# Five pairs with seven products in 13 of 15 linears of a decoder layer, with all their weight sums read from memory

## The chip, the cores and the metric

The kernel runs on one core of one Trainium2 chip. The metric is the device time of one execution, in microseconds (us). The engines are named as in the profile: PE is TensorE (matmuls; PEld its weight loads), DVE is VectorE, ACT is ScalarE, POOL is GpSimd, SP is SyncE. SP issues most DMA transfers on one queue (q1, hardware), POOL issues on another (q0, software).

## The reference

One decoder layer over 272 tokens (16 meta tokens and 256), width D = 2048, in fp32: a SwiGLU feed-forward part with F = 5632, then differential attention and a short convolution side by side, merged by gates, then a second SwiGLU part, then a norm. Cut to what matters:

```python
def swiglu_ffn(h, w_gu, w_down):
    gate, up = jnp.split(h @ w_gu, 2, axis=-1)
    return (jax.nn.silu(gate) * up) @ w_down

s = s + 0.5 * swiglu_ffn(rms_norm(s, norm_ffn1), ffn1_w_gu, ffn1_w_down)
h = rms_norm(s, norm_mix)
q, k, v, b_gate, c_gate, u = jnp.split(h @ w_in, splits, axis=-1)
y_att, y_conv = diff_attention(q, k, v, ...), short_conv_mixer(b_gate, c_gate, u, conv_w)
z = jnp.einsum('blnw,nwd->blnd', jnp.stack([y_att, y_conv], axis=2), w_branch)
s = s + jnp.sum(sigmoid(h @ w_gate) * z, axis=2) @ w_out
s = s + 0.5 * swiglu_ffn(rms_norm(s, norm_ffn2), ffn2_w_gu, ffn2_w_down)
return rms_norm(s, norm_final)[:, N_META:]
```

The weights come from HBM; by their shapes they are 394 MB.

## The kernel before

**Products.** A product of fp32 matrices is made of three matmuls: each operand is split in a high part, rounded to the type that PE takes (fp32r), and the rest. ACT makes the high part of a weight block ("wh", a cast), DVE subtracts it from the block ("wl"), and PE adds up activation-high x wh, activation-low x wh and activation-high x wl (`product`, L555 to L563). Pools: three buffers each of wh and wl (`W_BUFS`), eight of raw blocks of 512 KB (`ST_BUFS`, tag "st"), 28 of the activation tiles (`N_ACT`, tag "act"), eight of tiles for evictions (`ev`).

**Stages.** The first feed-forward part and w_in (to about 1130 us) run through `linear` (L311): one block of two 128-row chunks of weights after the other, 272 tokens wide, each with a load on SP, a cast, a subtraction and the matmuls. The steps of the attention are placed between blocks. Gates and branches (g, z, to about 1390), w_out (o, to about 1483) and the second feed-forward part run through `stream` (L664).

**stream.** It takes a list of slots. At each slot n it writes out the preparation of slot n + 2 (loads on SP, casts, subtractions), then the products of slot n, then steps hung on that slot, and then at most `room` steps from a list `todo` (evictions and the like, on DVE). DVE's instructions stay in the order in which they are written there (`Chain`, `dve`), so they wait for one another; SP's loads go in order too. PE's order is made by the scheduler.

**Two kinds of pairs.** The second feed-forward part is in three thirds of four, four and three groups of 512 columns of F. Each third has its "pg" linears (`w_gu`: 512 gate columns and 512 up columns of a group, together one product of 2x2 blocks) and two "pd" linears (`w_down`). A pg linear goes over eight pairs of 128-row chunks of weights (a pd linear of a third over eight or six). A pair is one of two kinds, by a letter in a string:

- D (`direct`, L565): two slots, 8 products, 24 matmuls of 128x512. Each slot loads 512 KB ("st").
- S (`mixed`, L594): four slots (raw, sums, sums2, single), seven products of sums of blocks in place of eight, 21 matmuls. It needs the raw left blocks "sr", one right block of "sx", and two tiles of sums of weights, "ta" and "tb". Sums of activations are made once ("xf", "ma", "mb", in `combine` and `combining`).

The strings are `HALF` (pg, four S), `TURNED` with `ORDER` (pd of the first two thirds, four S) and `SHORT` (pd of the last third, two S; the last linear of all is D throughout).

**Sums of weights.** ta and tb are made in one of two ways. On the spot: both blocks are loaded whole and DVE makes four additions of 128x512. Or from memory: a `Store` (L267) has made them long before, for a list of units, and the S pair loads ta and tb as it loads weights. In every string one S pair (the third in a linear) is summed on the spot; the others, 47 in all, are units. Beside these, the 12 S pairs of w_gate are summed on the spot.

**The Store.** `tick` is called once for each block of `linear`. Every sixth block (`STEP`) it loads a unit's two blocks "ur" and "un" (512 KB each) through SP into two st buffers, three blocks later it makes the four additions on DVE into two more st buffers "ua" and "ub", and POOL issues the two stores.

Of the kernel before, what the change touches and what calls it, by code (L numbers as in the profile page):

```python
# [9 lines left out]
F32 = mybir.dt.float32  # L10
# [5 lines left out]
P = 128  # L16
D = 2048
SEQ = 256
NMETA = 16
T = SEQ + NMETA  # L20
# [15 lines left out]
N_ACT = 28  # L36
# [6 lines left out]
HALF = "DDDSSDSS"  # L43
TURNED = "DSDSDSDS"
ORDER = (0, 2, 4, 1, 3, 6, 5, 7)
SHORT = "DDDSDS"
STEP = 6
# [4 lines left out]
def decoder_layer(ctx: ExitStack, tc: tile.TileContext, t, out):  # L52
# [54 lines left out]
    grow = const.tile([DC, P], F32, name="grow")  # L107
# [16 lines left out]
    vrows = const.tile([NV, P], F32, name="vrows")  # L124
# [11 lines left out]
    lamv = const.tile([P, 4, HD], F32, name="lamv")  # L136
# [34 lines left out]
    def make_lam():  # L171
        lprod = tmp.tile([P, 2, HD], F32, tag="lprod", bufs=1, name="lprod")
# [46 lines left out]
    class Norm:  # L219
# [5 lines left out]
        def add(self, c):  # L225
            first = self.ssq is None
            if first:
                self.ssq = tmp.tile([P, T], F32, tag="ssq", name="ssq")
            sq = self.ssq if first else tmp.tile([P, T], F32, tag="sq", name="sq")
# [4 lines left out]
        def end(self):  # L234
# [3 lines left out]
            ms = tmp.tile([P, T], F32, tag="ms", bufs=1, name="ms")  # L238
# [16 lines left out]
    def rsqrt(out_, ms, shape, name):  # L255

        a = tmp.tile([P, T], F32, tag="rsa", bufs=1, name="rsa" + name)[:, : shape[1]]
# [9 lines left out]
    class Store:  # L267


        def __init__(self):  # L270
            self.units, self.kept, self.count, self.v = [], {}, -DC // KB, None

        def want(self, w, r0, c0, c1):
            key = (w.tensor.name, r0, c0)
            self.kept[key] = [spill.tile([P, 2 * GW], F32, name=f"sums{len(self.kept)}{n}") for n in "ab"]
            self.units.append((w, r0, c0, c1, self.kept[key]))
# [4 lines left out]
        def tick(self):  # L281
            n = self.count % STEP
# [3 lines left out]
            if n == 0 and self.units:  # L286
                w, r0, c0, c1, _ = self.units[0]
                self.v = [raw_tile(n) for n in ("ur", "un")]
                for tl, cq in zip(self.v, (c0, c1)):
                    nc.sync.dma_start(  # L290
                        out=tl, in_=w[r0 : r0 + 2 * P, cq : cq + GW].rearrange("(c p) f -> p c f", p=P)
                    )
            if n == STEP // 2 and self.v:
                kept = self.units.pop(0)[-1]
                (r, x), self.v = self.v, None
                ta, tb = raw_tile("ua"), raw_tile("ub")
                added(nc.vector, r, x, ta, tb)
                for tl, to in zip((ta, tb), kept):
# [1123 lines left out]
```

## Time and profile before

| | us |
|---|---|
| median of 3 runs (2188.74 to 2189.27) | 2189.15 |
| the profiled execution, its own time | 2188.72 |
| its span, first to last instruction | 2186.9 |
| first feed-forward part and w_in, to about | 1130 |
| g and z, to about | 1390 |
| o, to about | 1483 |
| second feed-forward part, to about | 2160 |

The profiled execution lies 1.8 us above its span and 0.4 us below the median. In the profile "x9" counts instructions; a group of the page has its busy time, the mean of one in ns, and the idle time of the engine ahead of it with what ended that. Matmuls overlap, so that the length of one (some 0.39 us for 128x512) is not the time it takes of PE; that is read from the distance of starts. The name pgC stands for the accumulators C11, C12 and C21 of a pg linear, pgD for D22, pgP for P1, P5, P6 and P7, which only S pairs fill.

### The profile page before, as it was taken

To read this page: it belongs to the slowest core of one execution; us is meant where nothing else is said; L and a number is where in the kernel's file an instruction comes from. 1 tells how busy PE (TensorE), PEld (TensorE's weight loads), DVE (VectorE), ACT (ScalarE), POOL (GpSimd) and SP (SyncE) were. 2 spreads that over 40 slices of the span, in tenths; PEclk is the share of its full clock that TensorE was granted. 3 is DMA by queue.
4 is the path that set the end of the run, shared out by engine and by line. 5 is a ranking of instruction groups with operands and counts; after the bars stand their busy time and mean duration, and the time that the engine had idled before them with its cause. 6 is when DMAs were issued, how large, how long until landed. Compare 5 with 4: busy or idle time off the path is not lost.

```text
span 2186.9 us, 34858 instructions
## 1 busy us (share of the span) xinstructions
PE 2173.7 (99%) x13450; PEld 1955.7 (89%) x13450; DVE 1643.5 (75%) x2214; ACT 1109.3 (51%) x1431; POOL 60.6 (3%) x119
## 2 busy tenths in 40 slices
PE   9999999999999999999999999999999999999998
PEld 8999999999999999999988888888878888888886
DVE  7767665566766767666777787768888988888888
ACT  6434333333433444444445555556666566655665
POOL 0000000000000000000000000000000000000000
PEclk9999999999999999999999999999999999999999
DMA  7787888879888988744556665656777877878874
GB/s 238 263 309 275 294 295 288 301 261 317 302 276 287 320 294 303 260 145 135 167 162 212 212 207 190 211 180 216 250 239 258 280 238 259 273 244 277 282 244 154
DMA packets 240966, 542.09 MB, mean 248 GB/s; under 512 B 18564, under 2 KB 18624, under 8 KB 240800
## 3 DMA queue, kind: packets, MB, share of 16 engines
q1 hardware_dynamic: 225184, 484.25, 66.5%
q0 software_dynamic: 15232, 54.96, 6.7%
q8 instruction: 105, 1.72, 0.3%
q10 hardware_dynamic: 384, 0.66, 0.1%
q14 instruction: 61, 0.50, 0.1%
HBM read 486.18 MB, written 53.61 MB: 247 GB/s over the span
## 4 chain that ended last, share of the span: by engine, by line
PE 98%; ACT 1%; DVE 1%; DMA 1%; issue 0%; DVEq 0%
PE pgC L560 12%; PE pdC L560 7%; PE pgP L560 6%; PE gC L560 5%; PE pd L346 4%; PE pu L346 4%; PE pu L344 4%; PE pd L344 4%; PE pu L345 4%; PE pd L345 4%; PE pg L346 4%; PE pg L344 4%; PE pg L345 4%; PE zC L560 3%; PE o L709 3%; PE pgD L560 3%
## 5 line engine op out<-in xcount | busy, mean ns | idle before, releaser
L331 ACT CAST wh<-st 128x1024 fp32r<-128x1024 f32 x352 | 369.6, 1051 | 566.9 <-PE pd L345 134.8
L332 DVE TENSOR_TENSOR wl<-st,wh 128x1024 fp32r<-128x1024 f32 x352 | 429.6, 1222 | 273.8 <-ACT wh L331 273.2
L84 DVE TENSOR_TENSOR wl<-st,wh 128x1024 fp32r<-128x1024 f32 x246 | 299.3, 1220 | 85.2 <-ACT wh L504 78.2
L504 ACT CAST wh<-st 128x1024 fp32r<-128x1024 f32 x238 | 247.4, 1053 | 184.2 <-PE o L709 39.9
L344 PE MATMUL pg<-h,wh 128*128 128x272 f32 x704 | 202.8, 289 | 1.7 <-ACT wh L84 1.4
L344 PE MATMUL pu<-h,wh 128*128 128x272 f32 x704 | 203.2, 289 | 0.0
L346 PE MATMUL pd<-m,wl 128*128 128x272 f32 x704 | 203.0, 288 | 0.0
L346 PE MATMUL pu<-h,wl 128*128 128x272 f32 x704 | 203.0, 288 | 0.0
L344 PE MATMUL pd<-m,wh 128*128 128x272 f32 x704 | 203.0, 288 | 0.0
L345 PE MATMUL pu<-h,wh 128*128 128x272 f32 x704 | 202.4, 288 | 0.0
L345 PE MATMUL pd<-m,wh 128*128 128x272 f32 x704 | 202.4, 287 | 0.0
L345 PE MATMUL pg<-h,wh 128*128 128x272 f32 x704 | 201.4, 287 | 0.0
L346 PE MATMUL pg<-h,wl 128*128 128x272 f32 x704 | 199.7, 289 | 0.0
L560 PE MATMUL pgC<-wh,h 128*128 128x512 f32 x528 | 163.3, 391 | 0.0
L344 PEld LDWEIGHTS pg<-h,wh 128*128 128x128 f32 x704 | 132.3, 188 | 2.6 <-ACT wh L84 2.6
L504 ACT CAST wh<-ta 128x1024 fp32r<-128x1024 f32 x74 | 77.9, 1052 | 108.3 <-DVE ta L84 72.7
L345 PEld LDWEIGHTS pg<-h,wh 128*128 128x128 f32 x704 | 132.8, 189 | 0.0
L345 PEld LDWEIGHTS pu<-h,wh 128*128 128x128 f32 x704 | 132.7, 189 | 0.0
L345 PEld LDWEIGHTS pd<-m,wh 128*128 128x128 f32 x704 | 132.7, 189 | 0.0
L346 PEld LDWEIGHTS pu<-h,wl 128*128 128x128 f32 x704 | 132.5, 188 | 0.0
L346 PEld LDWEIGHTS pd<-m,wl 128*128 128x128 f32 x704 | 132.5, 188 | 0.0
L344 PEld LDWEIGHTS pu<-h,wh 128*128 128x128 f32 x704 | 132.2, 188 | 0.1
(479 smaller groups left out, 5162.0 us busy)
## 6 DMA issues: line engine op xcount, KB each, us to landing
st<-in_ffn_w_gu_dram SPq DMA_DIRECT2D x176, 512.0 KB, 5.9
st<-in_ffn_w_down_dram SPq DMA_DIRECT2D x140, 512.0 KB, 6.2
st<-in_w_in_dram SPq DMA_DIRECT2D x96, 512.0 KB, 4.4
st<-in_ffn_w_gu_dram SPq DMA_DIRECT2D x176, 256.0 KB, 4.3
sr<-in_ffn_w_gu_dram SPq DMA_DIRECT2D x44, 512.0 KB, 4.2
st<-in_w_gate_dram SPq DMA_DIRECT2D x40, 512.0 KB, 4.7
ur<-in_ffn_w_gu_dram SPq DMA_DIRECT2D x33, 512.0 KB, 7.8
un<-in_ffn_w_gu_dram SPq DMA_DIRECT2D x33, 512.0 KB, 5.0
```

Source lines behind the costliest of these rows:

```text
L84: r = f(*a, **k)
L331: act_.copy(out=wh[:, :m, :], in_=sw)
L332: dve_.tensor_sub(wl[:, :m, :], sw, wh[:, :m, :].bitcast(F32))
L344: nc.tensor.matmul(a, wh[:, i, f], act.part(c, 0, t0, t1), start=first, stop=False)
L345: nc.tensor.matmul(a, wh[:, i, f], act.part(c, 1, t0, t1), start=False, stop=False)
L346: nc.tensor.matmul(a, wl[:, i, f], act.part(c, 0, t0, t1), start=False, stop=last)
L504: nc.scalar.copy(out=wt[0][:, : sw.shape[1], :], in_=sw)
L560: nc.tensor.matmul(ps[:, f0:f1], x, wt[:, f0:f1], start=count[n] == self.whole[n], stop=count[n] == 1)
L709: nc.tensor.matmul(a, wh[:, i, f], act.both(c, 0, SEQ), start=first, stop=False)
```

## The change

Pairs: 14 pairs turn from D to S. `HALF` becomes `FIVE` ("DDDSSDSS" to "DDDSSSSS") for nine of eleven pg linears; in the linears of groups 7 and 10, `FOUR` keeps pair 5 as D. `TURNED` and `ORDER` change so that four pd linears end with five S pairs in a row, and `SHORT` gets a third S.

Sums: all S pairs of a linear are units, except in the linears with four S pairs, where the third is still summed on the spot (groups 7 and 10). So 74 units are stored instead of 47, and 2 of 76 S pairs of this part are summed on the spot instead of 15. The 12 of w_gate stay as they are.

The Store: a unit's loads are issued by POOL, not SP. Their two tiles come from the act pool during the first feed-forward part (its buffers go from 28 to 30) and from the st pool later. The four additions are made in place in these two tiles, over two ticks, 9 ticks after the load (4 in the later stages). Units begin 2 in 11 ticks in the first feed-forward part, 1 in 5 in the w_in linears, 1 in 6 in the slots of z and o, which tick now too. Both sums of a unit lie in one tensor in memory, written by two DMAs.

Other: the four slots of a stored S pair allow one step of `todo` each (`room` 0 to 1). Some small tiles move from the const and tmp pools to the ev pool.

```diff
-N_ACT = 28
+N_ACT = 30
-HALF = "DDDSSDSS"
-TURNED = "DSDSDSDS"
-ORDER = (0, 2, 4, 1, 3, 6, 5, 7)
-SHORT = "DDDSDS"
-STEP = 6
+FIVE = "DDDSSSSS"
+TURNED = "DSDSDSSS"
+ORDER = (0, 2, 4, 1, 3, 5, 6, 7)
+SHORT = "DDDSSS"
+RATES = ((2, 11), (1, 5), (1, 6))
+LAGS = (9, 4, 4)
+FOUR = {7: 5, 10: 5}
...
-        def tick(self):
-            n = self.count % STEP
+        def tile(self, name):
+            if self.stage == 0:
+                return apool.tile([P, 2, GW], F32, tag="act", name=name)
+            return raw_tile(name)
+
+        def next(self):
+            self.stage, self.count = self.stage + 1, 0
+
+        def tick(self, v=nc.vector):
+            num, den = RATES[self.stage]
+            now = self.count * num // den != (self.count - 1) * num // den
             self.count += 1
             if self.count <= 0:
                 return
...
+            for unit in self.begun:
+                unit[0] -= 1
+                if unit[0] in (0, -1):
+                    unit[1 - unit[0]](v)
+            self.begun = [u for u in self.begun if u[0] > -1]
+            if now and self.units:
+                self.begin(*self.units.pop(0))
+
+        def begin(self, w, r0, c0, c1, kept):
+            r, x = [self.tile(n) for n in ("ur", "un")]
+            for tl, cq in ((r, c0), (x, c1)):
+                nc.gpsimd.dma_start(
+                    out=tl, in_=w[r0 : r0 + 2 * P, cq : cq + GW].rearrange("(c p) f -> p c f", p=P)
+                )
+
+            def first(v):
+                v.tensor_add(r[:, 0, :], r[:, 0, :], x[:, 0, :])
+                v.tensor_add(x[:, 0, :], x[:, 1, :], x[:, 0, :])
+
+            def second(v):
+                v.tensor_add(x[:, 1, :], r[:, 0, :], x[:, 1, :])
+                v.tensor_add(r[:, 1, :], x[:, 1, :], r[:, 1, :])
+                nc.gpsimd.dma_start(out=kept[:, 1:3, :], in_=x)
+                nc.gpsimd.dma_start(out=kept[:, 0:4:3, :], in_=r)
+
+            self.begun.append([LAGS[self.stage], first, second])
...
             kept = store.get(self.w, (self.k0 + 2 * g) * P, self.c0)
+            room = 0 if kept is None else 1
...
-                Slot(raw, lambda: p((1, "P1", "r", 0), (2, "C11", "r", 1)), 0),
+                Slot(raw, lambda: p((1, "P1", "r", 0), (2, "C11", "r", 1)), room),
...
-    h3 = Pairs("h3", HALF)
+    h3 = Pairs("h3", FIVE)
```

Three places of the order. The first is DVE's order in a pg linear of the first third, from its first S pair on (wl<-sr, wl<-ta, wl<-tb and wl<-sx are the four subtractions of an S pair; m, ma, xf and mb belong to the activations of the next pd linear). Before:

```order
L84 TENSOR_TENSOR wl<-tb,wh 128x1024
L84 TENSOR_TENSOR wl<-sx,wh 128x512
L84 TENSOR_TENSOR wl<-sr,wh 128x1024
L84 TENSOR_TENSOR wl<-ta,wh 128x1024
L84 TENSOR_TENSOR wl<-tb,wh 128x1024
L84 TENSOR_TENSOR wl<-sx,wh 128x512
L84 TENSOR_TENSOR wl<-st,wh 128x1024 x2
L84 TENSOR_TENSOR wl<-sr,wh 128x1024
L84 TENSOR_TENSOR ta<-sr,sx 128x512
L84 TENSOR_TENSOR ta<-sx 128x512
L84 TENSOR_TENSOR mb_12969<-xf,mb_12969 128x512
L84 TENSOR_TENSOR tb<-ta,sx 128x512
```

With the change, from the same subtraction on:

```order
L86 TENSOR_TENSOR wl<-tb,wh 128x1024
L86 TENSOR_TENSOR mb_13030<-xf,mb_13030 128x512
L86 TENSOR_TENSOR wl<-sx,wh 128x512
L86 TENSOR_TENSOR wl<-sr,wh 128x1024
L86 TENSOR_TENSOR wl<-ta,wh 128x1024
L86 TENSOR_TENSOR wl<-tb,wh 128x1024
L86 TENSOR_TENSOR wl<-sx,wh 128x512
L86 TENSOR_TENSOR wl<-sr,wh 128x1024
```

The step "mb" has moved from the third S pair, among the sums on the spot, to the first; the direct pair (wl<-st x2) between the S pairs and the additions to ta and tb are gone, and the four subtractions repeat without a break for five pairs.

The second is PE's order in the same first S pair, from the third product of sums on (P6, then C21, then C12 with "single", then the next pair's first). Before:

```order
L560 MATMUL pgP_16977<-wh,h3b_12947 128x512 x2
L560 MATMUL pgC_16809<-wh,h3a_12946 128x512 x2
L560 MATMUL pgC_16805<-wh,h3b_12947 128x512 x2
L560 MATMUL pgP_16946<-wh,h3a_12948 128x512 x2
L560 MATMUL pgP_16977<-wl,h3b_12947 128x512
L560 MATMUL pgC_16809<-wl,h3a_12946 128x512
L560 MATMUL pgC_16805<-wl,h3b_12947 128x512
L560 MATMUL pgC_16801<-wh,h3a_12948 128x512 x2
```

With the change:

```order
L579 MATMUL pgP_17157<-wh,h3b_13007 128x512 x2
L579 MATMUL pgC_16989<-wh,h3a_13006 128x512 x2
L579 MATMUL pgC_16985<-wh,h3b_13007 128x512 x2
L579 MATMUL pgP_17124<-wh,h3a_13008 128x512 x2
L579 MATMUL pgP_17157<-wl,h3b_13007 128x512
L579 MATMUL pgC_16989<-wl,h3a_13006 128x512
L579 MATMUL pgC_16981<-wh,h3a_13008 128x512 x2
L579 MATMUL pgP_17137<-wh,h3b_13009 128x512
L579 MATMUL pgC_16985<-wl,h3b_13007 128x512
```

The wl product of the single block (C12, the third wl row before, the last row with the change) stands three matmuls later.

The third is POOL's order in the first feed-forward part with the change; before, POOL issued only the stores of a unit, and SP its two loads, after every six blocks of st:

```order
L310 DMA ur<-in_ffn_w_gu_dram 128x2x512
L310 DMA un<-in_ffn_w_gu_dram 128x2x512
L310 DMA ur<-in_ffn_w_gu_dram 128x2x512
L310 DMA un<-in_ffn_w_gu_dram 128x2x512
L310 DMA ur<-in_ffn_w_gu_dram 128x2x512
L310 DMA un<-in_ffn_w_gu_dram 128x2x512
L321 DMA sums_138<-un 128x1024
L322 DMA sums_138<-ur 128x2x512
L321 DMA sums_139<-un 128x1024
L322 DMA sums_139<-ur 128x2x512
L321 DMA sums_140<-un 128x1024
L322 DMA sums_140<-ur 128x2x512
```

The loads of three units stand together, then the six stores of these.

More of the change, by code (lines that the diff above doesn't have):

```diff
@@ L227, in add @@
             if first:
-                self.ssq = tmp.tile([P, T], F32, tag="ssq", name="ssq")
-            sq = self.ssq if first else tmp.tile([P, T], F32, tag="sq", name="sq")
+                self.ssq = ev([P, T], "ssq")
+            sq = self.ssq if first else ev([P, T], "sq")
             self.act.activation(sq[:, self.n0 :], s(c, self.n0), AF.Square)
@@ L285, in tick @@
                 return
[L286 to L298, printed above, removed]
-                    nc.gpsimd.dma_start(out=to, in_=tl.rearrange("p c f -> p (c f)"))
-    def added(v, r, x, ta, tb):
-        v.tensor_add(ta[:, 0, :], r[:, 0, :], x[:, 0, :])
-        v.tensor_add(ta[:, 1, :], x[:, 1, :], x[:, 0, :])
-        v.tensor_add(tb[:, 0, :], ta[:, 0, :], x[:, 1, :])
-        v.tensor_add(tb[:, 1, :], tb[:, 0, :], r[:, 1, :])
+            for unit in self.begun:
[20 more added lines that the diff above has]
+            self.begun.append([LAGS[self.stage], first, second])
     store = Store()
@@ L510, in decoder_layer, with __init__ @@
     class Mixed:
-        def __init__(self, act, pairs, w, k0, c0, c1, name, evict, steps=(), hold=0):
+        def __init__(self, act, pairs, w, k0, c0, c1, name, evict, steps=(), hold=0, but=None):
             self.act, self.w, self.k0, self.c0, self.c1, self.name = act, w, k0, c0, c1, name
-            self.kinds = ["D" if hold else act.kinds[g] for g in pairs]
+            self.kinds = ["D" if hold or g == but else act.kinds[g] for g in pairs]
             self.banks, self.count = {}, {}
@@ L570, in prep @@
                 sw = self.load(g, k)
+                if self.name == "z":
+                    store.tick(dve)
                 v[k] = new_w(kept)
@@ L975, in decoder_layer @@
         for g in third:
-            for k in in_store(HALF, range(8)):
-                store.want(w_gu, 2 * k * P, g * GW, F + g * GW)
+            want(FIVE, [k for k in range(DC // 2) if k != FOUR.get(g)], w_gu, 0, g * GW, F + g * GW)
         kinds, order = (TURNED, ORDER) if whole else (SHORT, range(6))
         for u in range(2 if whole else 1):
-            for k in in_store(kinds, order):
-                store.want(w_down, (third[0] * GC + 2 * k) * P, u * W2, u * W2 + GW)
+            want(kinds, order, w_down, third[0] * GC, u * W2, u * W2 + GW)
     before1 = First()
@@ L1147, in att_out @@
         return f
+    store.next()
     for g in range(2):
@@ L1336, in decoder_layer @@
             linears.append(
-                Mixed(h3, range(DC // 2), w_gu, 0, g * GW, F + g * GW, "pg", Gated(gi, norm3, mt), steps)
+                Mixed(h3, range(DC // 2), w_gu, 0, g * GW, F + g * GW, "pg", Gated(gi, norm3, mt), steps,
+                    but=FOUR.get(g))
             )
@@ L1395, in decoder_layer @@
             turns = []
+    store.next()
     stream(linears)
+    assert not store.units and not store.begun
 _INS = [
```

41 lines of the change are left out of this document (23 added, 18 removed).

## The prediction

> **What bounds the kernel now.** I read the page from the top: busy time, then the chain of work that ended last, then stretches of the span, and last the places where the matrix engine stops.
>
> ```profile
> span 2186.9 us, 34858 instructions
> PE 2173.7 (99%) x13450; PEld 1955.7 (89%) x13450; DVE 1643.5 (75%) x2214; ACT 1109.3 (51%) x1431; POOL 60.6 (3%) x119
> q1 hardware_dynamic: 225184, 484.25, 66.5%
> PE 98%; ACT 1%; DVE 1%; DMA 1%; issue 0%; DVEq 0%
> ```
>
> TensorE (PE) is busy for 99% of the span and makes 98% of the chain. Nothing is won by taking work off another engine; the time falls only by as many matmuls as go away, less what makes PE wait that didn't before. The next view, busy time by stretch, says who could become such a reason (columns: length, busy us of PE, PEld, DVE, ACT, POOL, then granted clock, DMA share, GB/s).
>
> ```profile
> 20.00:940.00 920.00, 918.29 (x7179) 906.77 (x7178) 625.61 (x870) 387.29 (x488) 52.17 (x98) 1.00 0.83 285
> 940.00:1130.00 190.00, 190.00 (x1395) 175.49 (x1394) 132.13 (x265) 87.50 (x173) 0.00 (x0) 1.00 0.51 154
> 1130.00:1390.00 260.00, 259.73 (x1147) 212.72 (x1146) 204.26 (x234) 139.96 (x156) 2.12 (x4) 1.00 0.62 205
> 1483.00:2160.00 677.00, 676.88 (x3006) 549.71 (x3005) 590.22 (x703) 424.87 (x500) 1.05 (x2) 1.00 0.76 255
> ```
>
> The clock is full everywhere. In the last row, the second feed-forward part where the change removes matmuls, PE is full, but DVE is at 590/677 = 87%. So this is a part in which DVE is second in line.
>
> How long one matmul takes is read from starts, not from durations, since they overlap. The chain has these pieces in one "pg" linear and the next two (start, length):
>
> ```profile
> 1528.82 2.04 PE pgC L560 x9
> 1531.54 2.04 PE pgC L560 x9
> 1534.26 2.04 PE pgC L560 x9
> 1536.98 2.04 PE pgC L560 x9
> 1540.14 2.09 PE pgC L560 x9
> 1582.57 2.09 PE pgC L560 x9
> 1624.97 2.09 PE pgC L560 x9
> ```
>
> The first four are one slot of a direct pair each, 12 matmuls of 128x512, 2.72 us apart: 2.72/12 = 0.227 us each. The last three begin the same slot of three linears: 42.4 us for one. A direct pair (D, 24 matmuls) takes 5.44 us of PE, a pair of seven products (S, 21) 4.76 us.
>
> **What goes.** 14 pairs turn from D to S: one in each of nine "pg" linears, one in each of five "pd" linears. That is 42 matmuls: 42 x 0.227 = **-9.5 us**. This term is sure, as nothing else on PE is added.
>
> The sums on the spot go too (all but two). What they cost today stands in the list of PE's waits for weights, over the whole span and in one linear (total us, times, longest):
>
> ```profile
> PEld pgP L560 <- DVE wl L84: 4.8, 15, 0.4
> PEld pgC L560 <- DVE wl L84: 2.1, 7, 0.3
> PEld pdP L560 <- DVE wl L84: 1.8, 6, 0.4
> PEld pdC L560 <- DVE wl L84: 0.9, 3, 0.3
> PEld pgP L560 <- DVE wl L84: 0.6, 2, 0.3
> PEld pgC L560 <- DVE wl L84: 0.3, 1, 0.3
> ```
>
> The lower two rows are the linear from 1540 to 1583: three waits, a pgP and the pgC at its first S pair, and one pgP after the pair that is summed on the spot. So the pgC and pdC rows count the linears with a late first pair (10), and the surplus of pgP and pdP over them, 15 - 7 + 6 - 3 = 11 waits of 0.3 us, belongs to the sums on the spot. What a wait for weights costs PE itself is read from its starts, here around the first S pair's two waits of 0.6 us:
>
> ```profile
> 1547.31 0.61 PE L560 MATMUL pgP<-wh,h3a 128*128 128x512 f32 x2
> 1548.75 0.62 PE L560 MATMUL pgC<-wh,h3a 128*128 128x512 f32 x2
> ```
>
> Five matmuls start from the first row to the second (two in the first, three single ones between): 1.44 us where 5 x 0.227 = 1.14 would do, so 0.3 us are lost, half of the wait, since matmuls were still running. I take nine waits at 0.15: **-1.3 us** (bounds 0 and -3.3).
>
> **What comes.** DVE's rhythm in two S pairs, from the timeline of DVE (start, length):
>
> ```profile
> 1545.55 1.07 DVE L84 TENSOR_TENSOR xf<-xf 128x256 f32<-128x256 f32 x3
> 1546.54 1.22 DVE L84 TENSOR_TENSOR wl<-tb,wh 128x1024 fp32r<-128x1024 f32 x1
> 1547.68 0.68 DVE L84 TENSOR_TENSOR wl<-sx,wh 128x512 fp32r<-128x512 f32 x1
> 1548.28 1.22 DVE L84 TENSOR_TENSOR wl<-sr,wh 128x1024 fp32r<-128x1024 f32 x1
> 1552.29 2.35 DVE L84 TENSOR_TENSOR wl<-st,wh 128x1024 fp32r<-128x1024 f32 x2
> 1556.90 0.68 DVE L84 TENSOR_TENSOR mb<-xf,mb 128x512 fp32r<-128x512 f32 x1
> L504 ACT CAST wh<-ta 128x1024 fp32r<-128x1024 f32 x74 | 77.9, 1052 | 108.3 <-DVE ta L84 72.7
> ```
>
> A pair whose sums are read costs DVE 1552.29 - 1548.28 = 4.0 us, PE 4.76 us. So DVE gains 0.75 us in every S pair; today it uses this to catch up in the second pair of two. With five in a row it has longer to catch up, but it also no longer gets the direct pairs behind it, which cost it 2.3 us and PE 5.4.
>
> *First S pair of a linear.* The addition "mb" (0.6 us from start to start) stands in the order of DVE today after both S pairs; with the change it stands between "wl<-tb" and "wl<-sx" of the first pair, which is where PE waits already. Unhidden it costs 0.6 us in each of ten linears, 6 us. But PE's order was changed with it: there the "wl" products of that pair are put behind more "wh" products, so that PE has work meanwhile. I take 0.1 x 10 = **+1.0 us**, nearer to the hidden end, as half of a late load was hidden even where the order did nothing for it (bounds 0 and 6).
>
> *Five S pairs in a row.* Each piece of weights passes a cast on ACT (1.05 us), the subtraction (1.14 us start to start) and six matmuls (1.36 us) in one of three buffers: 3.55 us and the hand-overs. Five pairs need four pieces in 4.76 us, so a buffer turns in 3 x 4.76/4 = 3.57 us on average. That is almost no slack, and it holds only because two of PE's six matmuls wait for "wl" and the fourth piece is half as large. Where a piece is late, I expect one wait like today's: 0.15 us of PE in 13 linears, **+2.0 us** (bounds 0, and 0.75 us in each, the whole of DVE's gain in a pair, 9.8).
>
> *Transfers.* A stored S pair loads 1.835 MB (sr, ta, tb 512 KB each, sx 256 KB) in 4.76 us, 385 GB/s; a direct pair 193. The rows of the DMA view between 1547 and 1562, where four such loads were issued within 3 us (GB/s in 40 slices; KB and us to landing):
>
> ```profile
> GB/s 0 0 0 0 16 104 71 208 377 388 404 410 404 344 71 71 87 131 251 279 306 377 366 377 366 350 426 415 350 350 186 109 55 38 104 98 377 366 388 246
> sr<-in_ffn_w_gu_dram SPq DMA_DIRECT2D x2, 512.0 KB, 4.6
> ta<-sums5a SPq DMA_DIRECT2D x1, 512.0 KB, 6.0
> tb<-sums5b SPq DMA_DIRECT2D x1, 512.0 KB, 6.6
> sx<-in_ffn_w_gu_dram SPq DMA_DIRECT2D x1, 256.0 KB, 6.1
> ```
>
> Full slices carry 350 to 426 GB/s; over the whole span the queue moved 484.25 MB in 66.5% of 2186.9 us, 333 GB/s at full share. So 385 is about what the engines can do. But only three of the five pairs are loaded inside the run: with eight buffers of "st" the first two lie ready when it begins. A buffer comes free when the subtraction has read it, at 1548.28 + 1.22 = 1549.5 for the sr above. That one's cast began 1.05 us before the subtraction at the latest, at 1547.2, so the cast two pairs on is due 2 x 4.76 us later, at 1556.7: 7.2 us for a load that landed in 4.6 to 6.6 us. I cost the transfers at nothing beyond the +2.0; the cover is 0.6 to 2.6 us, and what its loss costs is the second rival.
>
> The Trainium skill's page "DMA: Bandwidth & Descriptors", section "Where 436 GB/s comes from", puts the limit for transfers from HBM at about 358 GB/s for a core, which speaks against five such pairs: by it a pair would take 5.13 us, 0.37 us too long, and three pairs 1.1 us, some of it beyond the cover; 13 linears would lose at most 14 us. The slices above 400 GB/s disagree with it for stretches of 2 us, and the measurement decides.
>
> *Linears that share the buffers.* In the third stage two of eight "st" buffers are taken by a stored unit for some 45 us at a time in three of the gate linears, whose sums are still made on the spot: **+0.5 us** (bounds 0 and 3 x 2 pairs x 0.6 = 3.6).
>
> *The units.* 47 become 74, four additions each:
>
> ```profile
> L302 DVE TENSOR_TENSOR ua<-ur,un 128x512 f32<-128x512 f32 x47 | 32.5, 691 | 22.3 <-DMA un<-in_ffn_w_gu_dram 11.8 <-DMA un<-in_ffn_w_down_dram 9.6
> SPq L325 <- DVE ub L304: 186.4, 46, 8.5
> ur<-in_ffn_w_gu_dram SPq DMA_DIRECT2D x33, 512.0 KB, 7.8
> ```
>
> In the first feed-forward part the rate hardly changes (2 in 11 blocks for 1 in 6), and DVE is at 68% there. The new ones fall to the 96 blocks of w_in, 19 at one in five, and to z and w_out, 10. From 940 to 1130 (55 such blocks) 11 units x 4 x 0.6 = 26 us are added to DVE's 132 of 190 us: 84%. The attention's steps wait for DVE there, a burst of two additions delays one by 1.2 us, and PE has other blocks to do meanwhile: **+0.5 us** (bounds 0 and 11 x 0.3 = 3.3). The loads leave SP's queue, which today is held 186.4 us by the units' buffers; PE waited for none of it, so that wins nothing. They land after 8 us and get nine blocks, 27 us.
>
> **Sum** against the profiled execution's own 2188.72 us: -9.5 - 1.3 + 1.0 + 2.0 + 0.5 + 0.5 = -6.8. The median shown is 0.43 higher, 2189.15, so the forecast is **2182.3 us**.
>
> **Rivals.** (1) *The gain is given back in the S runs:* three "w" buffers and "mb" make PE lose 0.6 us in each of 13 linears, 7.8 us where the sum has 1.0 + 2.0: 2187.1. For it: the turn of a buffer is 3.55 of 3.57 us. Against: two S pairs in a row run today with 0.3 us lost. (2) *The run is bound by transfers,* the case on the other side: at 333 GB/s five pairs take 27.5 us for 23.8 of PE; if loads land later than the 7.2 us, 3.7 less some 1.5 of cover, 2.2 us, is lost in each of 13 linears, 29 us, and the time is 2189 - 11 + 29 = 2207, slower. It decides where the landing of a load in the run passes 7.2 us. For it: 385 GB/s needed. Against: slices of 400, and two pairs loaded ahead. (3) *The units' bursts take the engines from the weights in the first part:* six loads are issued together, 3.1 MB. If queues share evenly, the weights get 167 GB/s where they need 0.524 MB in 3.05 us, 172; 19 us of that leave them 0.6 us behind, times some 15 bursts 9 us, about 2188. Against: eight blocks, 24 us, lie ahead of need, no longer shared with units. The even sharing is what the Trainium skill states in "DMA: Bandwidth & Descriptors", section "Queues, rings and completion order" (each DMA engine takes turns between queues packet by packet); no run here shows it yet. (4) *It doesn't do what it says:* DVE or the buffers hold the units up, their sums are late, and loads of ta wait: I see no sign, since units stand in order of use and the first is read 1460 us in.
>
> **How the numbers follow.** Forecast 0.62, rival 1 0.18, rival 2 0.10, rival 3 0.05, rival 4 0.02, and a gain above 11 us 0.03. A measurement of this kernel tells 0.2%, 4.4 us, from no change. Faster (below 2184.8) takes the forecast and the large gain, less 0.01 at the forecast's edge: **0.64**; within 0.2%: rivals 1 and 3, that edge and a little of 2: **0.26**; slower: the rest of rivals 2 and 4: **0.10**. The range goes from the sum with the good ends, about -11.5, to rivals 1 and 3 with the first losses of 2: **2177.5 to 2191**.
>
> **What would show it.** Right: 13323 matmuls of PE and a pg linear of 41.7 us (42.4 - 0.68); waits for "wl" once or twice per linear and none longer than 0.4 us; transfers of ta and tb in the runs landing within 7 us; DVE under 90% from 940 to 1130 with PE full. Wrong: PE idle in the fourth or fifth S pair while ACT waits for ta, tb or sx (rival 2); more waits for "wl" at every S pair (rival 1); PE short in the first 940 us with ACT waiting for st (rival 3).

## The result, and the profile after

| | us |
|---|---|
| forecast, with its range | 2182.3 (2177.5 to 2191) |
| before, median of 4 runs | 2188.94 (2188.71 to 2189.27) |
| changed, median of 4 runs | 2274.18 (2270.17 to 2278.88) |
| ratio, with its 95% interval | 1.039 (1.0366 to 1.0414): slower |

The change made the kernel 3.9% slower, where a gain of 0.3% was forecast. The page of the changed kernel, in the lines that answer to those of before (busy time, transfer queues, chain):

```profile
span 2275.0 us, 35371 instructions
PE 2201.1 (97%) x13408; PEld 1965.8 (86%) x13408; DVE 1705.2 (75%) x2313; ACT 1144.3 (50%) x1470; POOL 213.5 (9%) x321
q1 hardware_dynamic: 204928, 456.19, 59.2%
q0 software_dynamic: 44320, 160.87, 19.6%
PE 39%; DMA 5%; DVE 3%; issue 3%; ACT 1%; POOL 0%; DVEq 0%; POOLq 0%; ACTq 0%; SPq 0%
```

PE has 42 matmuls less, as the change says (13408 recorded for 13450), and yet is busy for 27 us more, and 74 us of the span it is idle where it was idle for 13. The chain, which was PE in 98% of the span, now has transfers, DVE and "issue" (time for which the view names no waiting) in it. Its shares add up to 51% only, as the view follows it back no further than 1090 us, so PE's 39% is not to be set against the 98%. So PE now waits, and it is slower where it works.

Where it waits shows when the stages are laid beside each other. This table is worked out from the start of the first matmul of each stage in the two traces (the last row ends with the last matmul):

| stage | before | changed | difference |
|---|---|---|---|
| start to first matmul of a linear | 8.6 | 9.9 | +1.3 |
| gate and up, first half | 300.6 | 300.4 | -0.1 |
| down, first half | 144.6 | 162.7 | **+18.1** |
| gate, up and down, second half | 361.6 | 361.6 | 0.0 |
| w_in | 314.6 | 371.5 | **+57.0** |
| g and z | 258.5 | 267.8 | **+9.2** |
| o | 94.8 | 94.4 | -0.4 |
| second feed-forward part | 695.1 | 697.8 | **+2.7** |

The pairs sit in the last row alone. They were to bring 9.5 us there and cost 2.7. Some 84 us come from three stages in which no matmul was changed: only units are made there. Not all of it is waiting, as the stretches of the first down linears and w_in in the changed kernel show (columns as in the prediction):

```profile
310.40:473.10 162.70, 150.59 (x1155) 148.92 (x1154) 95.40 (x116) 51.68 (x50) 32.88 (x48) 0.97 0.88 310
834.70:1206.20 371.50, 332.58 (x2276) 305.27 (x2276) 247.70 (x456) 145.40 (x266) 50.76 (x74) 0.94 0.73 244
```

In w_in PE is idle for 39 us, and the same matmuls keep it busy for 332.6 us where they took 314.6: the granted clock is 0.94 there and was 1.00 before. So 18 of the 57 us are matmuls at a lower clock. In e1 and e5 below, where the waits are gone, the clock is 1.00 in w_in again.

Who is waited for in these stages is asked of DVE, from 300 to 1300 us (columns: who, for whom, total us, times, longest):

```profile
DVE ur L315 <- DMA un<-in_ffn_w_down_dram: 54.3, 11, 9.4
DVE ur L315 <- DMA un<-in_ffn_w_gu_dram: 31.6, 10, 7.2
DVE ur L315 <- issue: 14.9, 4, 4.2
DVE ur L315 <- DMA sums<-un: 5.5, 2, 3.2
```

L315 is the first of the four additions of a unit. 27 times DVE stands before it until the loads have come, 106 us in all (all 27 waits end within 0.2 us of the landing of "un", also the six that the view puts down to something else). They lie in the first down linears (9 of 12 units, 28 us) and between 820 and 1176 us, which is w_in but for one of them (18 times, 78 us); in g and z no unit's addition waits. How one such wait looks is shown by the timelines of DVE and of POOL at a place in w_in (start, length, idle time ahead of it and what ended it):

```profile
869.41 1.23 DVE L351 TENSOR_TENSOR wl<-st,wh 128x1024 fp32r<-128x1024 f32 x1 [0.45 <-ACT wh L350]
879.75 0.69 DVE L315 TENSOR_TENSOR ur<-ur,un 128x512 f32<-128x512 f32 x1 [9.12 <-DMA un<-in_ffn_w_down_dram]
864.88 0.57 POOL L321 DMA_DIRECT2D sums<-un  x1 [9.58 <-DVE un L319]
865.60 0.71 POOL L322 DMA_DIRECT2D sums<-ur  x1
871.64 0.73 POOL L310 DMA_DIRECT2D ur<-in_ffn_w_down_dram  x1 [5.33 <-DMA sums<-un]
872.62 0.73 POOL L310 DMA_DIRECT2D un<-in_ffn_w_down_dram  x1 [0.25 <-issue]
```

DVE is done with a weight block at 870.6 and comes to the addition. At that time the load isn't even issued: POOL issues it at 871.6 and 872.6, when the store of the unit before has landed. DVE does nothing for 9.1 us, and the subtraction of the next block stands behind the addition. In PE's waits over the same stages it is that subtraction which is named, or, in the attention, another instruction of DVE (sc):

```profile
PE aT L1124 <- DVE sc L1116: 13.0, 3, 7.7
PE pd L365 <- DVE wl L351: 12.1, 7, 4.2
PE v L365 <- DVE wl L351: 7.6, 2, 5.7
```

Two readings are open. The third POOL row suggests that a unit's round trip (load, additions, store, the next load into the same buffers) takes longer than the time between units. Or the addition stands too early in DVE's order, and the trip would be covered if DVE did something else first.

### The profile page after: what moved, and what is told of

Read it like the earlier page. It is cut to its first block, busy times and chain, and to the rows that moved or that the text cites. A ratio compares the mean times of both kernels' runs of the same rounds, so it can differ in the third digit from the quotient of the medians.

```text
span 2275.0 us, 35371 instructions
## 1 busy us (share of the span) xinstructions
PE 2201.1 (97%) x13408; PEld 1965.8 (86%) x13408; DVE 1705.2 (75%) x2313; ACT 1144.3 (50%) x1470; POOL 213.5 (9%) x321
## 4 chain that ended last, share of the span: by engine, by line
PE 39%; DMA 5%; DVE 3%; issue 3%; ACT 1%; POOL 0%; DVEq 0%; POOLq 0%; ACTq 0%; SPq 0%
PE pgC L579 10%; PE pgP L579 6%; PE pdC L579 5%; PE gC L579 3%; PE o L732 3%; PE pgD L579 2%; PE pdP L579 2%; PE zC L579 2%; PE o L733 1%; DMA un<-in_ffn_w_gu_dram 1%; PE pdD L579 1%; PE gP L579 1%; DVE wl L86 1%; DMA st<-in_w_branch_dram 1%; PE gD L579 1%
## 5 line engine op out<-in xcount | busy, mean ns | idle before, releaser
L350 ACT CAST wh<-st 128x1024 fp32r<-128x1024 f32 x352 | 370.2, 1053 | 610.1 <-PE pd L364 153.0
L351 DVE TENSOR_TENSOR wl<-st,wh 128x1024 fp32r<-128x1024 f32 x352 | 429.6, 1223 | 251.7 <-ACT wh L350 251.1
L86 DVE TENSOR_TENSOR wl<-st,wh 128x1024 fp32r<-128x1024 f32 x218 | 265.9, 1222 | 69.6 <-ACT wh L523 63.3
L523 ACT CAST wh<-st 128x1024 fp32r<-128x1024 f32 x210 | 219.9, 1055 | 180.6 <-PE o L732 35.4
L365 PEld LDWEIGHTS pd<-m,wl 128*128 128x128 f32 x704 | 134.3, 191 | 13.8 <-DVE wl L351 13.7
L364 PEld LDWEIGHTS pd<-m,wh 128*128 128x128 f32 x704 | 134.5, 191 | 0.0
L363 PEld LDWEIGHTS pd<-m,wh 128*128 128x128 f32 x704 | 134.1, 190 | 0.0
L523 ACT CAST wh<-ta 128x1024 fp32r<-128x1024 f32 x88 | 92.8, 1055 | 81.0 <-DVE ta L86 36.9
```

The lines of the kernel that those rows point to most:

```text
L86: r = f(*a, **k)
L350: act_.copy(out=wh[:, :m, :], in_=sw)
L351: dve_.tensor_sub(wl[:, :m, :], sw, wh[:, :m, :].bitcast(F32))
L363: nc.tensor.matmul(a, wh[:, i, f], act.part(c, 0, t0, t1), start=first, stop=False)
L364: nc.tensor.matmul(a, wh[:, i, f], act.part(c, 1, t0, t1), start=False, stop=False)
L365: nc.tensor.matmul(a, wl[:, i, f], act.part(c, 0, t0, t1), start=False, stop=last)
```

## The experiments

Theories T (the round trip), H (the additions stand too early) and others are named in the expectations. The first eight kernels were profiled once each. Five of them leave the second feed-forward part as it is in the changed kernel; these and the changed kernel took 694.6 to 700.3 us for it, so differences of some 3 us there say nothing by themselves.

### Additions that wait for no load

```diff
+            same = ones.rearrange("p (o f) -> p o f", o=1).to_broadcast([P, GC, P])
+            away = self.stage > 0
+            def dry(v):
+                d = ev([P, GC, P], "dry")
+                v.tensor_add(d, same, same)
+                v.tensor_add(d, d, same)
...
             def first(v):
+                if away:
+                    return dry(v)
```

(and the same in `second`)

> In w_in, z and o the four additions of a unit are made on a resident tile, as many and as long, so that DVE does the same work but doesn't wait for the unit's loads; the loads and stores stay (the stored sums are the raw blocks there, so the output is not the reference's). Changed kernel: w_in takes 371.5 us (314.6 before), z and g 267.8 (258.5). Theory T (round trip): a unit's load waits for buffers that the unit before still holds for its store, load + additions + store take 18 to 20 us, more than the 15.1 us of five blocks, and DVE, in order, waits for the load at the additions. It expects w_in at 315 to 326 us, g and z at 258 to 262, the whole at 2205 to 2222 us. Rival D (DVE has too much work beside the attention): nothing changes, w_in stays at 365 or more. Rival M (the units' traffic slows the weights): w_in stays at 350 or more, with ACT waiting for st.

Measured: w_in 314.9 us, g and z 259.2, the whole 2213.42 (one run beside 2188.6). So neither DVE's work nor the traffic costs more than 0.3 us in w_in; the wait for the load, with the lower clock that came with it, is the 57 us. Theories D and M are out. T and H are not told apart by it, since both go through that wait. The loss in g and z is gone too, but by another way: no addition waits there. In the changed kernel ACT waits for weights in that stage:

```profile
ACT wh L523 <- DMA st<-in_w_branch_dram: 24.9, 10, 6.1
```

The units' tiles come from the same ring of eight st buffers as these weights, and SP's loads stand there until a unit's store has landed (19.5 us, 4 times). In e1, where the stores wait for no addition, ACT's wait is 4.2 us. That the ring is the way is a reading of these rows; the run with tiles of their own, below, bears on it.

### Fewer units in w_in

```diff
-RATES = ((2, 11), (1, 5), (1, 6))
+RATES = ((1, 5), (1, 7), (1, 6))
```

> One number changed: units begin every 5 blocks in the first feed-forward part (2 in 11 in the changed kernel) and every 7 in w_in (5). Theory T: 7 blocks are 21.1 us, above the round trip of 18 to 20 us, so DVE finds its loads landed: w_in at 315 to 328 us. Rivals D and M: the loss in w_in goes with the number of units, 14 for 19, so 57 us becomes 42 and w_in takes about 357. The first down linear, which lost 18 us, may lose more, since more units are asked of that part: 18 to 25.

Measured: w_in 336.1 us, the first down linears 162.4, the whole 2238.72. That is neither T's 328 or less nor the 357 of a price per unit. A miss for T in its numbers: 21.1 us between units are more than its round trip, and DVE still waited in w_in, before 11 of 13 units, 44 us. The first down linears lost 17.8 us, just under the 18 to 25 expected.

### The loads on SP again

```diff
-                nc.gpsimd.dma_start(
+                nc.sync.dma_start(
```

> Only the queue of the units' loads is changed back: SP issues them, not POOL. Theory T: the buffers are the same, so the round trip stays, and now SP's weights stand behind a load that waits for a buffer: w_in stays above 355 us and the first down linear above 155 (162.7 in the changed kernel, 144.6 before). Rival Q (POOL's order: a unit's load stands behind the stores of the unit before, which wait for DVE): both losses go, w_in 315 to 330, first down linear 145 to 148, the whole at 2200 or below.

Measured: w_in 358.9, first down linears 169.1, and the gate and up linears lose 3.6 and 4.1 us that they didn't lose before; the whole 2272.01. Rival Q is out: the queue on which the loads go is not the cause, though w_in is 12.6 us shorter than in the changed kernel and the first down linears 6.4 longer.

### The additions bound to their place in DVE's order

This asks T against H directly. A dependency without a wait keeps an addition behind the subtraction of the block at which the program text has it:

```diff
-            dve_.tensor_sub(wl[:, :m, :], sw, wh[:, :m, :].bitcast(F32))
+            store.at = dve_.tensor_sub(wl[:, :m, :], sw, wh[:, :m, :].bitcast(F32))
...
+        def pin(self, a):
+            if self.stage < 2:
+                tc.add_manual_dep(
+                    a.ins, self.at.ins.name,
+                    mybir.DependencyInfo(mybir.DependencyClass.NoSync, mybir.DependencyReason.DATA), reason="pin",
+                )
...
-                v.tensor_add(r[:, 0, :], r[:, 0, :], x[:, 0, :])
+                self.pin(v.tensor_add(r[:, 0, :], r[:, 0, :], x[:, 0, :]))
```

(and the same for the third addition)

> Only DVE's order is changed, in the first feed-forward part and w_in: the first and the third addition of a unit are bound behind the subtraction of the block at which they are written (9 or 4 blocks after the load is written, then one more), where the scheduler of the changed kernel puts them as early as it likes, every two or three blocks in the first down linear. No wait is added. Theory H (the additions stand too early in DVE's order): the first down linear goes from 162.7 us (144.6 before) to 145 to 148. For w_in theory T (the round trip through shared st buffers) says that the order doesn't matter: 350 us or more. If H held there too, w_in would come to 330 or less. Rival R (the act tiles make the same round trip in the first down linear): it stays at 158 or more.

Measured: the first down linears 144.6 us, w_in 317.1, the whole 2209.41. Nothing else was touched: the same buffers, rate, queue and bytes. T expected w_in at 350 or more and falls; H holds in both stages. What moved is seen in DVE's order in the first down linears. In the changed kernel the scheduler has put the units' additions (L315, L316, L319, L320) two blocks apart:

```
L315 TENSOR_TENSOR ur<-ur,un 128x512
L316 TENSOR_TENSOR un<-un 128x512
L319 TENSOR_TENSOR un<-ur,un 128x512
L351 TENSOR_TENSOR wl<-st,wh 128x1024
L320 TENSOR_TENSOR ur<-un,ur 128x512
L351 TENSOR_TENSOR wl<-st,wh 128x1024
L315 TENSOR_TENSOR ur<-ur,un 128x512
```

With the additions bound (L322, L323, L326, L327), six blocks lie between, which is the rate of 2 in 11:

```
L322 TENSOR_TENSOR ur<-ur,un 128x512
L323 TENSOR_TENSOR un<-un 128x512
L358 TENSOR_TENSOR wl<-st,wh 128x1024
L326 TENSOR_TENSOR un<-ur,un 128x512
L327 TENSOR_TENSOR ur<-un,ur 128x512
L358 TENSOR_TENSOR wl<-st,wh 128x1024 x5
L322 TENSOR_TENSOR ur<-ur,un 128x512
```

The list of DVE's waits from 300 to 1240 us of this kernel begins so:

```profile
DVE wl L358 <- ACT wh L357: 205.0, 177, 2.9
DVE wl L86 <- ACT wh L530: 20.8, 20, 4.3
DVE oN L1147 <- PE po L1146: 13.3, 14, 1.8
```

The additions are not in it. Set side by side from the starts in the traces, 95 in a hundred units had 17 us or more here from the issue of "un" to the first addition, and 95 in a hundred loads landed within 13.8 us (median 8.3). In the changed kernel a quarter of the additions began 7.4 us or less after the issue, where the median load took 9.4. Counted in DVE's order, 0 or 1 subtractions of weight blocks stood between that issue and the addition in w_in of the changed kernel, and 2 in most of the first down linears; with the additions bound there were 5 to 11 and 11 to 18, and no addition waited. So POOL's wait for the store was real, but in this kernel it cost nothing where DVE had subtractions ahead of the addition. The 9 us of g and z are left (267.9): the additions are not bound there, and none waits there.

### Tiles of their own for the units

```diff
-            if self.stage == 0:
-                return apool.tile([P, 2, GW], F32, tag="act", name=name)
-            return raw_tile(name)
+            return apool.tile([P, 2, GW], F32, tag="act", name=name)
...
-LAGS = (9, 4, 4)
+LAGS = (9, 9, 6)
```

(on top of the bound additions)

> As e5_pinned, and units take their two tiles from the act pool in all stages, not from the st ring that the weights run through, with lags of 9, 9 and 6 blocks. Theory T with H: DVE finds its loads landed everywhere: first down linear 145 to 148 us, w_in 315 to 323, g and z 258 to 262; with the second feed-forward part as in the changed kernel (697.8) the whole comes to 2191 to 2202. Rival D (the additions are too much work for DVE beside the attention) was answered by e1_dry_adds; rival M (traffic: units at 140 GB/s beside weights at 172) would keep w_in above 330.

Measured: w_in 316.8, g and z 258.9 (267.9 with the additions bound alone), the whole 2200.97. So the 9 us of z came from the st ring or the short lag. The run changes both, but the trace points to the ring: ACT's wait for the weights of the branches, 24.9 us in the changed kernel, is gone, though the lag is longer. But the first linears took 304.4 us in place of 300.4 (304.6 with the additions bound alone). The stretches of the first gate linear, of before, of this kernel and of e9 below (length, busy us of PE, PEld, DVE, ACT, POOL, clock, DMA share, GB/s) show why:

```profile
8.60:43.40 34.80, 33.08 (x230) 28.95 (x231) 26.86 (x48) 23.36 (x49) 0.00 (x0) 1.00 0.77 253
9.70:48.40 38.70, 34.95 (x233) 30.96 (x231) 25.84 (x48) 23.33 (x48) 2.58 (x4) 0.96 0.85 302
9.80:43.00 33.20, 32.77 (x235) 29.52 (x234) 26.30 (x48) 23.57 (x49) 0.00 (x0) 1.00 0.77 261
```

In the middle row POOL is at work: three units' loads have nothing to wait for and go out between 6 and 12 us, beside the first weights, for which ACT then waits twice, up to 3 us. The clock is 0.96 in that row, so a part of the 3.9 us is again matmuls at a lower clock (PE busy 1.9 us more). This is rival 3 of the prediction, at the start of the kernel only.

### Half the bytes of the sums

Now the second feed-forward part.

```diff
-                    nc.sync.dma_start(out=ta, in_=kept[0])
+                    nc.sync.dma_start(out=ta[:, 0:1, :], in_=kept[0][:, 0:1, :])
+                    ta = v["ta"] = ta[:, 0:1, :].to_broadcast([P, 2, GW])
```

(and the same for tb)

> In the S pairs of the second feed-forward part ta and tb are loaded by half, and cast and subtraction read that half twice (as many instructions of the same size; the output is not the reference's, since the second half of both sums is wrong). A stored S pair loads 1.31 MB in place of 1.835, 275 GB/s in place of 385. That part takes 697.8 us in the changed kernel, of which 685.5 would be left if only the matmuls of before less 42 and its waits counted. Theory B (transfers): the waits of PE for wh and wl from the third S pair on go, 0.5 to 1 us in each of 13 linears: 686 to 692. Rival W (three w buffers, ACT and DVE): the waits stay, 695 to 699.

Measured: 689.0 us, 8.8 less than in the changed kernel and 5.6 less than the lowest of the six runs with the same code. Theory B holds: the bytes of the sums cost at least half of the 9.5 us that the pairs bring. Five S pairs in a row in the changed kernel, the view of transfers between 1636 and 1652 us (KB, us to landing), and busy time by stretch in three such runs of pairs:

```profile
tb<-sums SPq DMA_DIRECT2D x2, 512.0 KB, 7.5
sx<-in_ffn_w_gu_dram SPq DMA_DIRECT2D x2, 256.0 KB, 7.5
sr<-in_ffn_w_gu_dram SPq DMA_DIRECT2D x1, 512.0 KB, 7.2
ta<-sums SPq DMA_DIRECT2D x1, 512.0 KB, 7.9
1636.00:1649.00 13.00, 12.71 (x57) 10.00 (x56) 11.07 (x12) 9.25 (x11) 0.00 (x0) 1.00 0.95 335
1678.00:1691.00 13.00, 13.00 (x58) 10.55 (x57) 11.83 (x12) 9.71 (x11) 0.00 (x0) 1.00 0.95 323
1721.00:1736.00 15.00, 14.64 (x65) 11.67 (x64) 12.61 (x14) 10.65 (x12) 0.00 (x0) 1.00 0.96 342
```

The DMA engines are at 95%, and the loads land in 7.2 to 7.9 us, at and past the 7.2 us that the prediction had as the point of decision. These are the late ones: over the whole part the medians are 5.5 us for ta and 6.0 for tb. With half the sums the engines are hardly less busy in such stretches (92 to 95% in 13 to 15 us from 1632, 1674 and 1716 us, with PE full), so the share of busy time is not the mark; the medians of ta and tb fall to 3.9 and 4.1 us. PE's waits for weights in that part, of the changed kernel (first four rows) and with half the sums (last two):

```profile
PEld pgP L579 <- DVE wl L86: 8.0, 19, 1.0
PEld pgP L579 <- ACT wh L523: 5.0, 15, 0.4
PEld pdP L579 <- DVE wl L86: 3.8, 8, 1.0
PEld pgC L579 <- DVE wl L86: 2.0, 5, 0.4
PEld pgP L579 <- ACT wh L523: 4.6, 14, 0.4
PEld pgP L579 <- DVE wl L86: 2.2, 7, 0.3
```

With fewer bytes the pgP waits for wl fall from 8.0 to 2.2 us and the longest from 1.0 to 0.3. The short waits for wh stay: those are not of the transfers.

### Where the S pairs stand

```diff
-FIVE = "DDDSSSSS"
+FIVE = "DDSSDSSS"
-ORDER = (0, 2, 4, 1, 3, 5, 6, 7)
+ORDER = (0, 2, 1, 3, 4, 5, 6, 7)
-FOUR = {7: 5, 10: 5}
+FOUR = {7: 2, 10: 2}
```

> Only the places of the S pairs in the second feed-forward part are changed: a direct pair stands between the second and the third S pair (D D S S D S S S in place of D D D S S S S S). The matmuls, the units and the bytes are the same. That part takes 697.8 us from its first matmul to the last (695.1 before; 685.5 if only the matmuls had gone). Theory B (transfers: in the run of five a load lands 7 to 8 us after its issue and is late from the third pair on): the waits after the third pair go, 0.5 to 1 us per linear in 13, so 685 to 692. Rival W (three w buffers and the added step mb, whatever the transfers do): 696 to 699, with waits at each S pair.

Measured: 694.9 us, between both expectations and within the scatter of the same code, so inconclusive as a whole. The trace shows two things that offset each other: PE's waits for wl at pgP were fewer (4.1 us for 8.0), but in three of the four pg linears of the first third PE lost 0.56 us at the step from the second S pair to the direct pair, where the turns of the activations (xf, ma on ACT) now fell among S pairs. That these turns are the cause was not tried.

### mb one pair later

```diff
-            room = 0 if kept is None else 1
+            self.nth = getattr(self, "nth", 0) + 1
+            room = 1 if kept is not None and self.nth > 1 else 0
```

> Only the steps between slots are changed: the first S pair of a linear allows none (the changed kernel allows one per slot), the later ones one as now. In DVE's order mb moves from the first S pair to the second. The waits at the first S pair cost PE about 0.5 us per linear in the changed kernel and 0.3 before. Theory P (mb costs there): 10 linears x 0.2, so the second feed-forward part goes from 697.8 to 694.5 to 696.5. Rival (mb is hidden by PE's order, or costs as much one pair later): 697 to 699.

Measured: 692.9 us, 4.9 less than the changed kernel and 1.7 below the lowest of the same code. The three groups of pg linears took 167.1, 166.4 and 124.2 us where the changed kernel had 170.6, 168.1 and 124.5. PE's waits at pgP bear it out. Of the two rows shown above for the changed kernel, the one for wh (5.0 us, 15 times) is gone, and the one for wl is less than half:

```profile
PEld pgP L579 <- DVE wl L86: 3.3, 10, 0.5
```

So mb in the first S pair costs, some 0.2 to 0.5 us in each of ten linears; the exact size is lost in the scatter. e11 below has the same code in this part and took 691.6.

### All together

e9 takes the bound additions, the units' own tiles, mb one pair later, the spread order of the pd linears alone (pg as in the change), and holds the first three units back:

```diff
+            if len(self.units) + 4 > self.total:
+                for tl in (r, x):
+                    self.pin(nc.vector.memset(tl[:, 0, 0:1], 0.0))
```

> e7_own_tiles with three more edits: the first units' loads wait for a one-column write by DVE behind the block at which they are written (in e7_own_tiles six loads of 512 KB went out at 6 to 12 us and the first linear lost 4 us to them); mb in the second S pair (as e8_mb_later); the order of pairs of the pd linears D D S S D S S S (as in e4_spread, pg as it is). Theories H and B together: first linears 300 to 301 us after a start at 8.6 to 9.5, first down linear 144.6, w_in 315 to 318, pg as in e8_mb_later (457 to 459 for the three thirds), pd as in e4_spread (230 to 232), the whole at 2182 to 2187, 0.1 to 0.3% faster than before. If the small tiles in the ev pool and not the units' loads hold up the start, it stays at 9.7 or later. If more waits show in pd, as with mb moved (235.2 in e8_mb_later), 2188 to 2191.

> e9_all_mended with units every 5 blocks in the first feed-forward part and every 7 in w_in (2 in 11 and every 5 there), so 14 for 19 in w_in. e7_own_tiles lost 2.2 us in w_in against before. If that is DVE's work beside the attention, 5 units less give 0.5 to 1 us; the first part is not touched, since DVE waits for nothing there: 0 to 1 us faster than e9_all_mended.

> e9_all_mended without the new order of pairs in pd: five S pairs in a row again in four pd linears. Theory B: the transfers are late there (512 KB of sr, ta, tb and 256 KB of sx per pair against 385 GB/s), so the pd linears of the first two thirds take 169 to 172 us together where e9_all_mended has 165 to 166: 3 to 6 us slower. If W held (buffers), they are alike within 1 us.

Ten runs of each, beside 25 of before (2189.15):

| | median us | ratio to before, 95% interval | second part, profiled run |
|---|---|---|---|
| e9, all | 2186.11 | 0.9986 (0.9977 to 0.9995) | 689.5 |
| e10, e9 with fewer units in w_in | 2184.65 | 0.998 (0.9971 to 0.9989) | 688.8 |
| e11, e9 with five S pairs in a row in pd | 2190.64 | 1.0007 (0.9997 to 1.0016) | 691.6 |

e10 is the fastest, 0.2% faster than before. w_in took 315.5 us in it and 316.8 in e9: five units less give 1.3 us there, a little more than the 0.5 to 1 expected. The order of the pd linears is worth 4.5 us between e11 and e9, where 3 to 6 were expected from the transfers; the four pd linears take 165.4 us in e9 and 168.1 in e11 in the profiled runs (169 to 172 were expected), so rival W with its 1 us is out. The first linears came to 298.5 us in e9, but began at 9.8 us still. The expectation took this as a sign for the small tiles that moved to the ev pool. e12 below speaks against it: it has these tiles in the ev pool as well, and begins at 8.6. What differs is PE's pace ahead of the first linear: six matmuls of a spare tile take 1.49 us in e9 and 0.83 in before and e12, and the trace's record of the full clock begins at 10.5 us in e9, at 6.0 in before and at 5.8 in e12. So the 1.2 us are matmuls at a lower clock; why the full clock comes later there stays open. Three stretches of e10, the first down linears, w_in and the second part:

```profile
308.70:453.30 144.60, 144.60 (x1154) 144.60 (x1154) 88.72 (x104) 51.55 (x50) 29.08 (x42) 1.00 0.94 330
815.80:1131.20 315.40, 315.40 (x2274) 291.53 (x2273) 241.54 (x443) 145.49 (x266) 42.22 (x62) 1.00 0.78 260
1484.60:2172.90 688.30, 687.28 (x3039) 555.40 (x3037) 600.18 (x713) 462.03 (x554) 1.13 (x2) 1.00 0.81 282
```

PE is full in the first two and idle for 1.0 us in the third.

### SP or POOL, once the order is right

e12 is e10 with the loads on SP, without the held-back first units.

> e10_fewer_in_w_in with the units' loads on SP's queue again, and without the one-column writes that hold the first of them back on POOL (on SP they stand behind the weights in order). With the order of the additions kept, theory H says that the queue of the loads is of no account: within 2 us of e10_fewer_in_w_in (2184.65). Rival Q (a queue of its own is worth something: on SP a load that waits for an act tile holds up the weights behind it): 5 us slower or more, with ACT waiting for st in the first feed-forward part.

Measured: 2185.71 us, ratio 0.9985 (0.9975 to 0.9994), against 2184.65: 1.1 us, with intervals that overlap. The queue is of no account that these runs could tell, and rival Q's 5 us are out.

## Why the prediction was wrong

**The step that failed** is the one on the units: "They land after 8 us and get nine blocks, 27 us." The landing was about right (9.4 us in the median of all units). The nine blocks were read from the program text, where the additions are written nine blocks after the load. For w_in, where most of the loss fell, even the text has four blocks (12 us), not nine. In the instruction order they stood where the scheduler had put them, mostly with 0 to 2 blocks between a load's issue and its addition, and DVE, which takes its instructions in order, came to them before the loads had landed, in w_in three times before one was even issued. The order in which POOL's loads and stores stood was quoted ahead of the prediction, but the distance of DVE's additions from them was not counted. With the additions bound to their blocks, 65 of the 85 us were gone at once (2274.18 to 2209.41). A part of what was lost, 18 of the 57 us in w_in, was a lower granted clock (0.94), where the prediction had "the clock is full everywhere" from the kernel before. Rival 4 had named the holder ("DVE or the buffers hold the units up") but asked only whether the sums would be late for their readers, 1460 us into the kernel. The price falls on what stands behind the waiting addition on DVE: the weights of the current block.

**The other terms**, by the runs:

- *Linears that share the buffers*, +0.5 with bounds 0 and 3.6: the cause was near and the size wrong. It was looked for in the gate linears; ACT waited for the branches' weights instead, and g and z lost 9.2 us. With other tiles and lags (e7) they take 258.9 for 258.5 before.
- The matmuls, -9.5 us: right. 42 fewer are recorded (13408; the prediction's sign of 13323 doesn't follow from the 13450 of its page), and in e10 the second part takes 688.8 us, 6.3 less than before, with some of the other terms still in it.
- *First S pair*, +1.0: the place was right, the size too small. Moving mb took 4.9 us off, less the scatter; the bound of 6 held. That PE's order hides most of it was not so. The -1.3 for the sums on the spot was not measured apart.
- *Transfers*, costed at nothing: the condition was right and the choice wrong. Rival 2 said that it decides where landing passes 7.2 us; 7.2 to 7.9 us were measured at 95% DMA share in one run of pairs. Half the sums gave 8.8 us back, 0.7 us for each of 13 linears, not the 2.2 that the rival had. The forecast's +2.0 for five pairs in a row stood for buffers of w; the runs show transfers in its place.
- The Trainium skill's page "DMA: Bandwidth & Descriptors", section "Where 436 GB/s comes from" (some 358 GB/s from HBM for a core), was set aside for slices of 400 GB/s. By the rates in the next item it was no limit of this kernel.
- *Rates*: the three stretches of S pairs above have 323 to 342 GB/s, but the changed kernel moved 371 GB/s over the 13 us from 1640, and e10 398 over the 20 us from 1968, loads alone, with PE full. So the loads of those stretches were late at a lower rate than the DMA engines reached elsewhere, and the runs don't show what set their time to landing.
- *Additions beside the attention*, +0.5: right. e1, with all of DVE's work but no waits for loads, has w_in at 314.9 us against 314.6; e9 has 316.8, 2.2 more, within the bound of 3.3.
- *The queue*, "that wins nothing": right (e12).
- Rival 3 (the units' bursts against the weights): seen only in the first 40 us, where it cost 4 us in e7. (Its 9 us on top of the forecast would be 2191, not 2188.) In e10's first down linears the DMA engines are at 94% and PE is full.
- Not thought of: the start, +1.3 us, at a lower clock.

**The sum** of the mended kernel is near the forecast, 2184.65 for 2182.3. The forecast was of a kernel whose additions stand where they are written. But e10 has other changes too (mb, the order in pd, the tiles and the rate), so that it comes near is no proof of the sum.

## What to carry to other kernels

A lag in the program text is no lag on the chip: where a scheduler orders an engine, count in that engine's order how many instructions stand between a transfer's issue and the first instruction that waits for it, and price what stands behind the waiting one. If an addition must come late, bind it to the work that is to cover it. And for a run of work that loads much, compare the time to landing with the time until a piece is due: neither the best slices of GB/s nor the share of busy time told here whether PE would wait.

## What the runs showed of the hardware

In the first down linears PE was full in e10 at a DMA share of 94% over 145 us (row above), where the changed kernel lost 18 us at 88% in the same stage: a busy queue was no reason by itself. Where PE waited much it was also slower: the granted clock was 0.94 in w_in of the changed kernel and 1.00 in e1 and e5 without the waits. By the trace's clock record it falls to 0.50 for 3.4, 6.8 or 10.2 us at a time, seven times in that stage. And the six profiled executions with the same code in the second part differ by 5.7 us there (694.6 to 700.3), while 25 whole executions of the kernel before lie within 1.95 us (2188.85 to 2190.8). A part of it is the clock: in three of the six (e1, e2, e7) it is 0.98 over the pd linears of the second third, which took 87.5 to 87.9 us there, where the three others have 1.00 and 85.3 to 86.5. What the rest of it is, and why the clock falls in some, was not tried.
